# Transformer trunk on one core: VectorE work ordered behind the convolution, and a mixture gather with the one-hot matrix stationary

## The chip, the core and the metric

The kernel runs on one core of a Trainium2 chip. The metric is device time in microseconds of one execution. Engines are named as in the profile: PE (TensorE), PEld (its weight load), DVE (VectorE), ACT (ScalarE), POOL (GpSimd), SP (SyncE, whose queue issues nearly all transfers). Everything is float32; "fp32r" is the reduced form of it that TensorE takes in one pass, and the kernel writes an fp32 value as a sum of two such parts, hi and lo, where one is not enough.

## The reference

Two layers over x (512 positions, 1024 channels). The first layer mixes by a Fourier group and a convolution group, the second by windowed attention; after each comes an expert-choice mixture. Every sub-layer starts with RMSNorm and a shift, scale and gate made from the conditioning vector c ("adaLN").

```python
def adaln(cond, w, b):
    shift, scale, gate = jnp.split(cond @ w + b, 3, axis=-1)

def fourier_conv_mixer(h, ...):              # layer 0
    proj = h @ w_in                          # u_f, u_v, u_g: 512 channels each
    y_f = real(fft2(u_f in 4 groups of 128)) # positions x channels
    glu = u_v * sigmoid(u_g)
    conv = depthwise_conv(glu, width 31) + conv_b
    y_c = silu(layer_norm(conv))
    return concatenate([y_f, y_c]) @ w_out

def ec_moe(h, ...):                          # both layers, 16 experts, 64 rows each
    aff = softmax(h @ router_w + router_b)
    gate, idx = top_k(swapaxes(aff), 64)     # each expert picks its 64 positions
    xg = h[idx]
    hid = silu(xg @ w_gate) * (xg @ w_up)    # 1024 x 1024 per expert
    return zeros.at[idx].add((hid @ w_down) * gate)

x = x + gate * mixer(h); x = x + gate * ec_moe(h)    # per layer, h = norm, scale, shift
```

## The kernel before

The program is unrolled Python. A scheduler orders each engine's queue from program order and its own estimate of durations. Two things override it: `behind(i)`, which puts the instructions traced inside it behind instruction i on the engine of i, and a manual order for PE that follows program order from the second pair of experts on.

**Slots.** Most transfers go to eleven buffers of 1 MiB ("w") and, at times, four more (3a, 3b, 4a, 4b), taken and given back in turn (`Slot`). SP's queue is in order, so a transfer whose buffer is not free holds up the ones behind it. "0a", "0b", "1a", "1b", "2a", "2b" are larger areas that several stages use one after another.

**Layer 0's mixer** (`mixer0`, L409) is written as a list of tokens (L616). Of these, `g` makes a gated input of the convolution (`gated`, L539), `c` a convolution of one of four 128-channel tiles (`conv`, L500), `F` and `s` the Fourier group, `D` and `E` an adaLN block (`ada_block`, or `ada_steps` if the token ends in d or p), `O` a half of the output weights split in hi and lo, `y` the hi and lo of one Fourier tile, `L`, `M`, `N` the LayerNorm over channels and swish, `e` and `m` the first and the second half of an output tile's matmuls, `B` the gate row, `T` the router's preparation (`Router(0)`), `r` its logits. The letter behind the dot is the engine that makes the lo parts: v for DVE, g for POOL.

**The convolution.** Tile 1 is made on ACT and POOL. Tiles 0, 3 and 2, in this order, are made on DVE: 31 taps each (L519, L522), every one a multiply-add of 128x512 that reads the running sum from a PSUM bank and writes it back. L then needs all four tiles: a sum over channels on PE (L602), the mean (L673), the subtraction (L675), squares, a second sum, the inverse root, and swish; then the lo and hi parts of the result (L588, L589) and the second halves of the output matmuls (L150 to L152).

**An adaLN block** multiplies c with 1024x512 weights on PE (L236), turns the row to columns (L296), adds them up on DVE (L298) and adds the bias on DVE (L299). `ada_steps` does the multiply on DVE or ACT and POOL instead, in eight steps (L275, L277) that are dealt out between the tokens that follow.

**The mixture** (`moe`, L905) takes experts in eight pairs. For a pair: gather the 128 rows (two experts of 64) through a one-hot matrix; gate and up (`expert_mm`, L1011), each 2 MiB a step in four steps; hid = silu(gate) * up, turned (L1118); down; combine (L1060: the transposed one-hot matrix times hi and lo of the result, added into x by DVE at L1063). While a pair's up is done, the next pair is gathered: `onehot` (L943) builds the 0/1 matrix on DVE and multiplies it by the norm's factor r on POOL (L955); `gather` (L959) takes 128x128 pieces of the frozen x ("0a", "0b") as the stationary operand and the one-hot matrix as the moving one, 32 fp32 matmuls of 128 columns, and scales and shifts each result (L972 on ACT, L974 on DVE) into one of two buffers "1b", "2b". `weights` (L977) turns the one-hot matrix for the combine (L983) and picks the affinities (L988). The expert weights of a layer are 16 x 3 x 4 MiB, read once.

## Time and profile before

| | us |
|---|---|
| median of 3 runs | 1469.9 |
| lowest and highest | 1465.23, 1471.7 |
| profiled execution, its own time | 1466.26 |
| its span in the trace | 1464.6 |

The span is taken from the first to the last instruction in the trace, and 1.7 us lie around it. Slices 8 to 18 (257 to 690 us) are the first mixture, 27 to 39 (985 us to the end) the second; before each stands a mixer, with PE, DVE, ACT and POOL at work on one chain of steps. An engine's busy share is a mean over these stages. PE's clock is printed as a share of 2.4 GHz; 0.5 is the lower of its two levels, 1.2 GHz.

### The profile page before, as it was taken

What the parts mean: (1) busy time and instruction counts of PE and PEld (TensorE: products, weight loads), DVE (VectorE), ACT (ScalarE), POOL (GpSimd) and SP (SyncE); (2) the same over time, 40 slices, a digit from 0 to 9 for tenths busy, and PEclk for the clock granted to TensorE, in tenths of its full rate; (3) what the DMA queues carried; (4) which work ended last, traced back from release to release, by engine and by line L of the source; (5) the groups of instructions that cost most, each with busy time, mean ns of one, the idle gap of its engine ahead of it and who ended that gap; (6) DMA issues with size and microseconds to landing.
All of it is one profiled execution on the core that took longest, in us unless ns stands there. A gap on an engine that the chain in (4) does not pass through costs nothing.

```text
span 1464.6 us, 18139 instructions
## 1 busy us (share of the span) xinstructions
PE 1361.0 (93%) x7235; PEld 771.0 (53%) x7235; DVE 593.3 (41%) x1170; ACT 337.1 (23%) x686; POOL 285.4 (19%) x234
## 2 busy tenths in 40 slices
PE   5999698999999999999798989979999999999995
PEld 3785475545455355354476666655454554553543
DVE  5589547121222212211477988671122222222214
ACT  3365232110010010010356543421100010010002
POOL 2488131200000000000256654410000000000002
PEclk8999797999999999999999989989999999999998
DMA  9469469979999999999800375688799999999995
GB/s 337 130 218 350 139 232 412 396 315 397 423 421 422 421 423 422 422 422 410 271 29 30 113 232 165 238 330 336 321 396 424 421 422 422 422 421 422 421 410 172
DMA packets 112860, 480.69 MB, mean 328 GB/s; under 512 B 10416, under 2 KB 31176, under 8 KB 67208
## 3 DMA queue, kind: packets, MB, share of 16 engines
q1 hardware_dynamic: 112696, 479.27, 82.9%
q8 instruction: 57, 0.93, 0.3%
q0 software_dynamic: 80, 0.26, 0.0%
q14 instruction: 27, 0.22, 0.0%
HBM read 477.40 MB, written 2.10 MB: 327 GB/s over the span
## 4 chain that ended last, share of the span: by engine, by line
PE 63%; DMA 20%; DVE 11%; ACT 3%; issue 1%; SPq 1%; POOL 1%; DVEq 0%; ACTq 0%; POOLq 0%
PE bank L1022 31%; PE bank L966 7%; DMA w<-in_moe_w_up_dram 5%; DMA w<-in_moe_w_gate_dram 5%; DMA w<-in_moe_w_down_dram 4%; PE bank L150 4%; PE bank L151 4%; PE bank L152 4%; PE bank L1060 3%; PE bank L1043 3%; PE bank L1352 1%; DVE bank L522 1%; PE bank L236 1%; DMA 4b<-in_moe_w_gate_dram 1%; DMA 4a<-in_moe_w_up_dram 1%
## 5 line engine op out<-in xcount | busy, mean ns | idle before, releaser
L1022 PE MATMUL bank<-w,area2b 128*64 128x512 f32 x736 | 187.0, 594 | 3.4 <-DMA w<-in_moe_w_up_dram 2.1
L1022 PE MATMUL bank<-w,area1b 128*64 128x512 f32 x704 | 181.7, 594 | 3.4 <-DMA w<-in_moe_w_up_dram 2.1
L1022 PE MATMUL bank<-w,area1a 128*64 128x512 f32 x632 | 161.5, 594 | 2.6 <-ACT area1a L162 1.2
L1063 DVE TENSOR_TENSOR x<-x,bank 128x512 f32<-128x512 f32 (+1 forms) x136 | 78.8, 650 | 176.1 <-PE bank L1060 176.1
L955 POOL TENSOR_TENSOR tmp<-tmp,rr 128x512 f32<-128x512 f32 x14 | 17.4, 1244 | 580.5 <-DVE tmp L949 558.8
L1022 PEld LDWEIGHTS bank<-w,area2b 128*64 128x64 f32 x736 | 62.3, 137 | 99.0 <-issue 85.2
L1022 PEld LDWEIGHTS bank<-w,area1b 128*64 128x64 f32 x704 | 60.3, 137 | 99.0 <-issue 85.0
L1053 DVE SCALAR_TENSOR_TENSOR tmp<-bank,af,gbc 128x512 f32<-128x512 f32 (+1 forms) x34 | 24.4, 719 | 211.5 <-PE bank L1022 184.7
L1113 DVE TENSOR_TENSOR area1a<-bank,area1a 128x512 f32<-128x512 f32 x32 | 22.0, 691 | 209.7 <-PE bank L1022 209.7
L128 POOL TENSOR_TENSOR w<-w,w 128x1024 fp32r<-128x1024 f32 x30 | 72.8, 2444 | 145.9 <-DMA 3b<-in_ada_w_dram 120.2
L1022 PEld LDWEIGHTS bank<-w,area1a 128*64 128x64 f32 x632 | 54.3, 137 | 76.1 <-issue 69.6
L1060 PE MATMUL bank<-area2a 128*128 128x512 f32 (+1 forms) x272 | 64.6, 387 | 6.4 <-ACT area2a L1054 6.4
L1054 ACT ACTIVATE area2a<-tmp 128x512 fp32r<-128x512 f32 (+1 forms) x34 | 20.6, 607 | 213.0 <-DVE tmp L1053 212.9
L1060 PEld LDWEIGHTS bank<-area2a 128*128 128x128 f32 x272 | 47.9, 188 | 30.3 <-ACT area1a L1089 9.7
L966 PE MATMUL bank<-tmp,0a 128*128 128x128 f32 x384 | 62.2, 285 | 0.0
L1089 ACT ACTIVATE area1a<-bank 128x512 f32<-128x512 f32 x32 | 19.1, 598 | 186.1 <-PE bank L1022 186.1
L966 PE MATMUL bank<-tmp,0b 128*128 128x128 f32 x384 | 61.0, 282 | 0.0
L150 PE MATMUL bank<-area1a,w 128*128 128x512 f32 x132 | 52.7, 418 | 5.8 <-ACT area1a L386 3.7
L966 PEld LDWEIGHTS bank<-tmp,0a 128*128 128x128 f32 x384 | 52.7, 196 | 9.7 <-issue 9.7
L972 ACT ACTIVATE area1b<-bank,mod 128x128 f32<-128x128 f32 x32 | 14.6, 457 | 179.1 <-DVE area1b L974 179.1
L152 PE MATMUL bank<-area1a,w 128*128 128x512 f32 x132 | 53.1, 404 | 1.2 <-POOL w L128 1.2
L151 PE MATMUL bank<-area2a,w 128*128 128x512 f32 x132 | 53.1, 402 | 0.1
(478 smaller groups left out, 2610.3 us busy)
## 6 DMA issues: line engine op xcount, KB each, us to landing
w<-in_moe_w_gate_dram SPq DMA_DIRECT2D x95, 1024.0 KB, 16.8
w<-in_moe_w_up_dram SPq DMA_DIRECT2D x85, 1024.0 KB, 19.7
w<-in_moe_w_down_dram SPq DMA_DIRECT2D x84, 1024.0 KB, 18.4
w<-in_ada_w_dram SPq DMA_DIRECT2D x42, 1024.0 KB, 5.7
4a<-in_moe_w_up_dram SPq DMA_DIRECT2D x10, 1024.0 KB, 12.3
3b<-in_moe_w_up_dram SPq DMA_DIRECT2D x10, 1024.0 KB, 17.1
3a<-in_moe_w_up_dram SPq DMA_DIRECT2D x9, 1024.0 KB, 15.6
4b<-in_moe_w_down_dram SPq DMA_DIRECT2D x9, 1024.0 KB, 16.1
```

Of the source, the lines that this page charges most:

```text
L128: eng.tensor_sub(lo.ap[:, s], w.ap[:, s], hi.ap[:, s].bitcast(FT))
L150: nc.tensor.matmul(ps, l[0], r[0], start=start, stop=False)
L151: nc.tensor.matmul(ps, l[0], r[1], start=False, stop=False)
L152: nc.tensor.matmul(ps, l[1], r[0], start=False, stop=stop)
L966: nc.tensor.matmul(p[:, P * q:P * q + P], src_x(t, 4 * hf + q), oh[:, P * t:P * t + P], start=t == 0, stop=t == TT - 1)
L1022: nc.tensor.matmul(ps[h][CAP * i:CAP * i + CAP], lhs[:, k, CAP * i:CAP * i + CAP], w[i].row(kk)[:, 512 * h:512 * h + 512], start=k == 0, s ...
L1043: nc.tensor.matmul(ps[CAP * i:CAP * i + CAP, :n], lhs[:, k, CAP * i:CAP * i + CAP], w[i][:, kk], start=k == 0, stop=k == KT - 1)
L1053: nc.vector.scalar_tensor_tensor(f, ps[:, :n], af, gbc[:, s], op0=OP.mult, op1=OP.mult)
L1054: nc.scalar.activation(Y[0][:, s], f, AF.Copy)
L1060: nc.tensor.matmul(p[:, :n], ohT[:, P * t:P * t + P], Y[z][:, c0:c0 + n], start=z == 0, stop=z == 1)
L1063: nc.vector.tensor_add(xx, xx, p[:, :n])
L1113: nc.vector.tensor_mul(sg[:, s], ps, sg[:, s])
```

## The change

Around the convolution, the blocks D1, D0, D2, D4, D5 and D3 no longer add their bias (`bias=False`). Two additions do it for all of them (`ada_bias`), at B and at T. These, the whole of `Router(0)` and the eight DVE steps of block E3 are put behind the convolution's last tap on DVE (`behind(*ended)`). The lo parts of O1, y3 and y2 go from DVE to POOL. Tile 2 is convolved ahead of tile 3.

In both mixtures, from the third pair on, the gather is `Rows`. During the up of pair n (n = 1 to 6), behind each of its four steps, PE multiplies the one-hot matrix of pair n+1 (now fp32r, and the stationary operand) with hi and lo of two 128x512 pieces of the frozen x, which ACT (hi) and DVE (lo) have just split. That is 16 matmuls of 512 columns. A half's sum is copied out of PSUM by ACT, turned by four PE transposes, and scaled and shifted as before. The first half is turned behind up, the second behind hid's transposes. The frozen x carries the factor r already, so POOL's multiplication of the one-hot matrix falls away. There is one buffer for the gathered rows of all pairs from the second on, and one for hid; "1b" and "2b" hold hi and lo.

```diff
-    def ada_block(l, s, j, room=None, fast=False):
+    def ada_block(l, s, j, room=None, fast=False, bias=True):
...
+    def ada_bias(l, s, c0, n):
+        m, b0 = mod[l, s][:, c0:c0 + n], 8 + (2 * l + s) * 24 + c0
+        return nc.vector.tensor_add(m, m, colsA[:, b0:b0 + n])
...
-                nc.vector.tensor_add(cv, acc, cv)
+                tap = nc.vector.tensor_add(cv, acc, cv)
+            ended[:] = [tap]
...
-        toks = ("p3 p0 p2 p1 p5 p4 g0 F0 g1 w:21 g2 s0:1 g3 D1:3 F2 F3 n F1 c0.0 D0:04 c1.30 c3.0 s2 D2:1 c2.0 s1 D4 "
-                "L D5:12 D3:22 s3:2 H O2.g:004 y0.g O0.g:033 M O1.v:01 N0.v y1.g O3.g y3.v y2.v N1.v e4 N2.v e0 e1 e3 "
+        toks = ("p3 p0 p2 p1 p5 p4 g0 F0 g1 w:21 g2 s0:1 g3 D1:3 F2 F3 n F1 c0.0 D0:04 c1.30 c2.0 s2 D2:1 c3.0 s1 D4 "
+                "L D5:12 D3:22 s3:2 H O2.g:004 y0.g O0.g:033 M O1.g:01 N0.v y1.g O3.g y3.g y2.g N1.v e4 N2.v e0 e1 e3 "
...
+        def after_conv(f):
+            def step():
+                with behind(*ended):
+                    f()
+            return step
...
-                drip += ada_steps(*(todo if op == 'D' else more)[j], arg == "p")
+                steps = ada_steps(*(todo if op == 'D' else more)[j], arg == "p")
+                drip += steps if arg == "p" else [after_conv(f) for f in steps]
...
-                ada_block(*todo[j], "0a" if arg else None)
+                ada_block(*todo[j], "0a" if arg else None, bias=False)
...
             elif op == 'B':
+                with behind(*ended):
+                    ada_bias(0, 0, 16, 8)
                 row_bcast(gbc, mod[0, 0][:, 16:24])
...
             elif op == 'T':
-                rt = Router(0)
+                with behind(*ended):
+                    ada_bias(0, 1, 0, 16)
+                    rt = Router(0)
...
-        hids = [kview(A1[:, 1024 + 1024 * i:2048 + 1024 * i]) for i in range(2)]
-        xgs = [kview(area(m, 1024)) for m in ("1b", "2b")]
+        hid = kview(A1[:, 2048:3072])
+
+        xgs = [kview(area("1b", 1024)), kview(A1[:, 1024:2048])]
...
+        class Rows:
...
+            def __init__(self, pr):
+                onehot(pr)
+                self.xg, self.oh = xgs[1], ohs[pr % 2]
+                if not stage:
+                    stage.extend(area(m, 1024, FR) for m in ("1b", "2b"))
+                self.rows = []
+
+            def step(self, c):
+                hf = c // 2
+                if c % 2 == 0:
+                    self.bank = Bank()
+                    self.p = self.bank.__enter__()
+                for t in range(2 * (c % 2), 2 * (c % 2) + 2):
+                    hi, lo = (stage[t % 2][:, 512 * z:512 * z + 512] for z in range(2))
+                    x = frozen[2 * t + hf]
+                    nc.scalar.activation(hi, x, AF.Copy)
+                    nc.vector.tensor_sub(lo, x, hi.bitcast(FT))
+                    for z, m in enumerate((hi, lo)):
+                        nc.tensor.matmul(self.p, self.oh[:, P * t:P * t + P], m, start=t + z == 0,
+                                         stop=t + z == TT)
+                if c % 2:
+                    f = tmp()
+                    nc.scalar.activation(f, self.p, AF.Copy)
+                    self.bank.__exit__()
+                    self.rows.append(f)
+
+            def turn(self, hf):
+                with Bank() as p:
+                    for q in range(4):
+                        nc.tensor.transpose(p[:, P * q:P * q + P], paired(self.rows[hf], q), ident)
+                    modulate(self.xg, p, hf, range(4))
...
-                expert_mm([u0, u1], xg, wu_d, e, None, None if pr else "u")
+                rows = None
+                if 0 < pr < NP - 1:
+                    rows = Rows(pr + 1)
+                expert_mm([u0, u1], xg, wu_d, e, None, None if pr else "u", rows and rows.step)
...
-                elif pr + 1 < NP:
-                    onehot(pr + 1)
-                    nxt = ahead()
+                elif rows:
+                    rows.turn(0)
+                    nxt = weights(pr + 1)
...
+            if rows:
+                rows.turn(1)
...
-                            nc.gpsimd.tensor_copy(frozen[2 * t + h], xx)
+                            nc.gpsimd.tensor_scalar(frozen[2 * t + h], xx, r, None, op0=OP.mult)
                         else:
-                            nc.scalar.activation(frozen[2 * t + h], xx, AF.Copy)
+                            nc.scalar.activation(frozen[2 * t + h], xx, AF.Copy, scale=r)
```

## Rows read from the trace of the kernel before

**Rows 1.** The page: busy time of each engine, and GB/s in 40 equal slices

```profile
PE 1361.0 (93%) x7235; PEld 771.0 (53%) x7235; DVE 593.3 (41%) x1170; ACT 337.1 (23%) x686; POOL 285.4 (19%) x234
...
GB/s 337 130 218 350 139 232 412 396 315 397 423 421 422 421 423 422 422 422 410 271 29 30 113 232 165 238 330 336 321 396 424 421 422 422 422 421 422 421 410 172
```

**Rows 2.** Windows inside the first mixture; busy time (instructions) by engine, clock, DMA share, GB/s

```profile
400.00:545.00 145.00, 143.83 (x776) 73.61 (x777) 33.80 (x58) 14.11 (x27) 4.07 (x3) 1.00 1.01 422
545.00:685.00 140.00, 135.11 (x672) 66.40 (x668) 30.02 (x52) 11.23 (x21) 1.06 (x1) 1.00 1.01 421
```

**Rows 3.** Chain of work that ended last, 540 to 720: start, length, what

```profile
545.97 19.77 DMA w<-in_moe_w_up_dram
...
685.88 3.66 PE bank L1022 x14
```

**Rows 4.** The same chain through one pair of experts, 395 to 470

```profile
399.76 7.74 PE bank L966 x64
407.50 0.44 PE bank L983 x4
...
410.24 27.69 PE bank L1022 x128
437.93 3.89 PE bank L1060 x16
441.82 13.88 PE bank L1022 x64
```

**Rows 5.** Windows where the weight stream has gaps

```profile
355.00:360.00 5.00, 5.00 (x26) 1.61 (x24) 0.00 (x0) 0.00 (x0) 0.00 (x0) 1.00 0.70 241
1090.00:1095.00 5.00, 4.57 (x22) 1.96 (x24) 0.33 (x1) 0.71 (x2) 0.00 (x0) 1.00 0.68 285
```

**Rows 6.** Timeline of DVE, 60 to 250: start, length, what, [idle before, releaser]

```profile
96.38 0.69 DVE L537 TENSOR_TENSOR 3b<-bank,tmp 128x512 f32<-128x512 f32 x1 [2.85 <-PE bank L152]
...
97.95 11.05 DVE L522 SCALAR_TENSOR_TENSOR bank<-3b,cw,bank 128x512 f32<-128x512 f32 x14
...
123.01 0.69 DVE L589 TENSOR_TENSOR area2a<-0a,area1a 128x512 fp32r<-128x512 f32 x1 [2.13 <-ACT area1a L588]
...
137.18 1.91 DVE L331 SCALAR_TENSOR_TENSOR a<-mod,colsC 128x4 f32<-128x4 f32 x1
...
139.67 1.90 DVE L763 TENSOR_TENSOR aw<-rw,a 128x128 f32<-128x128 f32 x1
...
160.33 0.75 DVE L522 SCALAR_TENSOR_TENSOR 0b<-3b,cw,bank 128x512 f32<-128x512 f32 x1
166.35 2.48 DVE L675 TENSOR_TENSOR 0b<-0b,bank 128x512 f32<-128x512 f32 x4 [5.27 <-PE bank L673]
```

**Rows 7.** Groups by line, DVE, 122.5 to 161.2: busy, mean ns, idle before

```profile
L275 DVE SCALAR_TENSOR_TENSOR w<-w,sil 128x512 f32<-128x512 f32 x6 | 4.5, 750 | 0.0
L331 DVE SCALAR_TENSOR_TENSOR a<-mod,colsC 128x4 f32<-128x4 f32 x2 | 2.6, 1282 | 0.0
```

**Rows 8.** Who waited for whom, 130 to 165

```profile
PE bank L602 <- DVE 0b L522: 12.2, 1, 12.2
```

**Rows 9.** Windows before and after the convolution's last tap (161.1), and around it

```profile
135.00:161.10 26.10, 10.34 (x47) 6.63 (x39) 25.86 (x37) 6.95 (x9) 6.29 (x4) 0.74 0.63 206
161.10:190.20 29.10, 27.27 (x126) 18.78 (x126) 7.67 (x20) 13.82 (x21) 8.35 (x7) 0.94 0.56 203
190.20:220.00 29.80, 29.80 (x167) 24.01 (x167) 14.58 (x20) 7.46 (x17) 10.55 (x8) 1.00 0.52 192
160.00:165.00 5.00, 3.87 (x9) 1.85 (x10) 1.04 (x2) 0.60 (x1) 0.00 (x0) 0.51 0.00 0
```

**Rows 10.** Timeline of POOL, 130 to 180

```profile
136.71 4.71 POOL L128 TENSOR_TENSOR w<-w,w 128x1024 fp32r<-128x1024 f32 x2
```

**Rows 11.** Instructions on tile tmp, 320 to 680: ns minimum/median/maximum

```profile
L1054 ACT ACTIVATE area2a<-tmp x12: 630/632/634, 368.3 to 655.1; 128x512 fp32r<-128x512 f32 x12
L1055 DVE TENSOR_TENSOR area2a<-tmp,area2a x12: 681/690/1530, 369.6 to 655.8; 128x512 fp32r<-128x512 f32 x12
```

More of the change, by code (lines that the diff above doesn't have):

```diff
@@ L255, in ada_block @@
                 nc.scalar.activation(rows, ps, AF.Copy)
-        return ada_cols(l, s, j, rows)
+        return ada_cols(l, s, j, rows, bias)
     def ada_steps(l, s, j, pool_too=False):
@@ L291, in ada_steps, with ada_cols @@
                 [lambda k=k: add(k) for k in range(4, 8)] + [finish])
-    def ada_cols(l, s, j, rows):
+    def ada_bias(l, s, c0, n):
+        m, b0 = mod[l, s][:, c0:c0 + n], 8 + (2 * l + s) * 24 + c0
+        return nc.vector.tensor_add(m, m, colsA[:, b0:b0 + n])
+    def ada_cols(l, s, j, rows, bias=True):
         with Bank() as pc:
@@ L296, in ada_cols @@
                 nc.tensor.transpose(pc[:, P * q:P * q + P], rows[:, P * q:P * q + P], ident)
-            b0, m = 8 + (2 * l + s) * 24 + 4 * j, mod[l, s][:, 4 * j:4 * j + 4]
-            nc.vector.reduce_sum(m, pc.rearrange("p (q g i) -> p q g i", q=4, g=4)[:, :, :, 0], axis=AX.X)
-            return nc.vector.tensor_add(m, m, colsA[:, b0:b0 + 4])
+            nc.vector.reduce_sum(mod[l, s][:, 4 * j:4 * j + 4],
+                                 pc.rearrange("p (q g i) -> p q g i", q=4, g=4)[:, :, :, 0], axis=AX.X)
+            return ada_bias(l, s, 4 * j, 4) if bias else None
     def ada(l, s, blocks):
@@ L521, in conv @@
                 else:
-                    nc.vector.scalar_tensor_tensor(out, g[:, k:k + S], wt(k), acc, op0=OP.mult, op1=OP.add)
+                    tap = nc.vector.scalar_tensor_tensor(out, g[:, k:k + S], wt(k), acc, op0=OP.mult, op1=OP.add)
             if split:
-                nc.vector.tensor_add(cv, acc, cv)
+                tap = nc.vector.tensor_add(cv, acc, cv)
+            ended[:] = [tap]
         todo = [(0, 0, 4), (0, 0, 5)] + [(0, 1, j) for j in range(4)]
@@ L530, in mixer0 @@
         tiles = [(w, P * j) for j in range(2) for w in w0] + [(wf0, P * j) for j in range(2)]
-        sum_bank = []
+        sum_bank, ended = [], []
         def glu_of(ct, pg, pv):
@@ L920, in moe @@
         sg = A1[:, 0:1024]
-        hids = [kview(A1[:, 1024 + 1024 * i:2048 + 1024 * i]) for i in range(2)]
-        xgs = [kview(area(m, 1024)) for m in ("1b", "2b")]
+        hid = kview(A1[:, 2048:3072])
+        xgs = [kview(area("1b", 1024)), kview(A1[:, 1024:2048])]
+        A2b = area("2b", 1024)
+        stage = []
         Y, ohTs = [], []
@@ L945, in onehot @@
             e = 2 * pr
-            ohs[pr % 2] = oh = tmp()
+            ohs[pr % 2] = oh = tmp(FR if pr > 1 else FT)
             if pr == 0:
@@ L959, in gather @@
         def gather(pr, hf):
[L961 removed]
+            xg, oh = xgs[pr], ohr[0]
             for qs in ((0, 1), (2, 3)) if pr == 0 else (range(4),):
@@ L965, in gather @@
                         for t in range(TT):
-                            nc.tensor.matmul(p[:, P * q:P * q + P], src_x(t, 4 * hf + q),
+                            nc.tensor.matmul(p[:, P * q:P * q + P], paired(x_sb[:, t], 4 * hf + q),
                                              oh[:, P * t:P * t + P], start=t == 0, stop=t == TT - 1)
-                    for q in qs:
-                        k = 4 * hf + q
-                        pp = p[:, P * q:P * q + P]
-                        if q % 2:
-                            nc.scalar.activation(xg[:, k], pp, AF.Identity, bias=sh[:, k:k + 1], scale=a[:, k:k + 1])
-                        else:
-                            nc.vector.tensor_scalar(xg[:, k], pp, a[:, k:k + 1], sh[:, k:k + 1],
-                                                    op0=OP.mult, op1=OP.add)
+                    modulate(xg, p, hf, qs)
@@ new lines, in modulate @@
+        def modulate(xg, p, hf, qs):
+            for q in qs:
+                k = 4 * hf + q
+                pp = p[:, P * q:P * q + P]
+                if q % 2:
+                    nc.scalar.activation(xg[:, k], pp, AF.Identity, bias=sh[:, k:k + 1], scale=a[:, k:k + 1])
+                else:
+                    nc.vector.tensor_scalar(xg[:, k], pp, a[:, k:k + 1], sh[:, k:k + 1], op0=OP.mult, op1=OP.add)
+        class Rows:
[28 more added lines that the diff above has]
+                    modulate(self.xg, p, hf, range(4))
@@ L977, in weights @@
         def weights(pr):
             e, oh, ohT = 2 * pr, ohs[pr % 2], ohTs[pr % 2]
-            o = [oh[:, P * t:P * t + P] for t in range(TT)]
+            o = [(oh.bitcast(FT) if pr > 1 else oh)[:, P * t:P * t + P] for t in range(TT)]
             with Bank() as p:
@@ L1009, in back, with expert_mm @@
                 pass
-        def expert_mm(ps, lhs, wd, e, middle=None, first=None):
+        def expert_mm(ps, lhs, wd, e, middle=None, first=None, after=None):
             for c in range(4):
@@ L1025, in expert_mm @@
                 back(w)
+                if after:
+                    after(c)
         def down_piece(ps, lhs, e, c0, n):
@@ L1091, in moe @@
                 combine_all(pend)
-            def ahead():
-                gather(pr + 1, 0)
-                gather(pr + 1, 1)
-                return weights(pr + 1)
             if pr == 0:
@@ L1130, in moe @@
             if pr == 0:
-                nxt = ahead()
+                gather(1, 0)
+                gather(1, 1)
+                nxt = weights(1)
                 frozen.extend(fourths("0a", "0b"))
```

11 lines of the change are left out of this document (4 added, 7 removed).

## The prediction

> **What bounds the kernel now.** Read the page first, then each stage by itself. The page has PE busy for 93% of the span, so a change that takes matmul time away looks as if it paid everywhere [rows 1]. The GB/s line beside it speaks against that: in both mixtures the transfers run at 421 to 423 GB/s for most slices and hardly ever above [rows 1]. So the second view is windows inside the first mixture. From 400 to 685 us the DMA share is 1.01 throughout, and PE's busy time is misleading: it stands at 143.8 of 145 and then 135.1 of 140 us, but the instructions per microsecond fall from 776/145 = 5.35 to 672/140 = 4.80 [rows 2]. The third view, the chain of work that ended last, says when that begins: from 546 on it runs through weight transfers of 19.8 us each, and PE works off what has just landed [rows 3].
>
> One pair of experts shows why. On PE a period goes from one gather to the next: 399.76 to 441.82 + 13.88 = 455.70, that is 55.94 us [rows 4]. The stream has to bring 24 MiB (2 experts, 3 matrices, 4 MiB each), 25.17 MB, which at 422 GB/s [rows 2] is 59.6 us. So DMA is the slower of the two by 3.7 us a pair; PE leads the chain only while the buffers, filled earlier, last. What counts in a mixture is therefore (a) when the stream starts and (b) where it has gaps.
>
> The other stage is the first mixer. There the view is the waits: PE stands for 12.2 us at the channel sum (L602) for DVE's last tap [rows 8], and from 135 to 161.1 us PE is busy 10.3 of 26.1 us while DVE is busy 25.9 [rows 9]. The timeline of DVE shows that it isn't only convolving there: between its taps stand router preparation (L331, L763), lo parts (L589) and E3's steps (L275) [rows 6, 7]. Here VectorE is the bound, and all that follows starts later for it.
>
> **The change: the convolution.** Taps run at 11.05/14 = 0.789 us each [rows 6]. The last two tiles need 62 of them, 48.9 us. In the trace the first of these tiles starts at 96.38 + 0.69 = 97.07, after 2.85 us of idleness for its gated input, and the last tap ends at 161.08 [rows 6]: 64.0 us for 48.9 us of taps. The other 15.1 us are what the change takes out: E3's eight steps (six of them 4.5 us), L331 2.6 [rows 7], L763 1.9, the lo parts of O1 (L128), L589 with its wait 2.8 [rows 6], and the bias additions, of the same kind as these small ones. Tile 2 ahead of tile 3 starts at once, at 93.53, since its input was made earlier. There remain the gated product of tile 3 (0.69) and six small sums, for which I take 1 us. So the last tap ends at 93.5 + 48.9 + 0.7 + 1.0 = 144.1, 17.0 us earlier.
>
> PE must be there to use it. Its 10.3 us of work between 135 and 161.1 [rows 9] stand ahead of the channel sum in its queue; without waits they end at 145.7. That is later than 144.1, so the sum starts 15.4 us earlier, not 17.0. Behind it PE is busy 27.3 of 29.1 us up to 190.2 [rows 9]: no cover is left there, and the whole of it moves as a block. The clock adds something: from 160 to 165 us the granted clock is 0.51, the lower level, behind a window in which PE was busy for 10.3 of 26.1 us [rows 9]; without such a pause the 3.9 us of matmuls in that window run at the higher level, worth up to 2 us.
>
> What was taken out must still be done. About 9 us of it (E3, L331, L763, two bias additions) goes to DVE behind the last tap. DVE is busy only 7.7 of the 29.1 us that follow [rows 9], and its first step on the chain, L675, has 5.3 us of idleness ahead of it [rows 6]. DVE's queue is in order, so each step of the chain can stand behind one moved step, 0.75 us [rows 7]; three such places cost 2.2 us, which I set against the clock. POOL gets O1's two lo parts (4.7 us, as the pair at 136.71 [rows 10]) and two Fourier tiles; it ends its own part of this stage at 141.4 [rows 10] and would end near 149, while the first matmuls on these come behind the LayerNorm. E3's transfers and buffers come at about the absolute time at which they came before. Sum: -15 us, between -8 (moved steps and POOL late at every place) and -20 (all of PE's 15.8 idle us, the clock, the 1.8 us at 190).
>
> Does it reach the end? From 190.2 to 220 us PE is busy without a pause [rows 9], with the output matmuls that need this chain's result, and the router and the first gather need theirs. The weight stream is no obstacle: it moves 206, 203 and 192 GB/s in these three windows [rows 9], half its rate, and waits for buffers that this stage holds. So both mixtures start earlier by the full amount.
>
> One row speaks against giving POOL more. L331 on 128x4 took 1.91 us and L763 on 128x128 took 1.90 us; both ended within 0.2 us of one of POOL's two subtractions, which fill 136.71 to 141.42 [rows 6, 10]. The Trainium skill ("SBUF — State Buffer", section "SBUF: two separate sides") gives a rule for it: VectorE and GpSimd share one pair of ports as an exclusive lock, so an operation of VectorE with two SBUF inputs blocks for the whole of GpSimd's. The trace agrees. By that rule E3's steps, which read two SBUF operands, would be held by O1's lo parts, and the sum would be -10 instead of -15; I don't take it, since taps, with one operand in PSUM, ran at 0.75 beside POOL.
>
> **The change: the gather.** Before, 7.74 us of PE a pair [rows 4]. After: 16 matmuls of 512 columns with an fp32r operand, as the combine's 16, 3.89 us, and eight transposes at 0.44 for four, 0.88 [rows 4]. So PE gains 2.97 us a pair, 12 times: 35.6 us in all. Nearly all of it is free time already: the stream takes 59.6 us where PE now takes 53.0. It pays only in the gaps of the stream behind the first new gather. There is one in each mixture, behind the second pair's up, when no buffer comes free during the gather: 0.30 and 0.32 of 5 us [rows 5], 1.5 and 1.6 us. Down now starts up to 3 us earlier, but the buffers of up are given back up to 2.9 us later, since three of the four steps stand between its matmuls. I take -2 for both mixtures, between 0 and -3.
>
> ACT and DVE get eight splits a pair, 0.63 and 0.69 us [rows 11], against 13.9 us of up [rows 4]; they run ahead of PE, with two sets of buffers. The waits that this adds (the first step behind the combine's additions, hid behind fewer matmuls) I put at 0 to 3 us a pair, inside the margin below.
>
> **The rivals.** (1) *PE is the bound and all its savings arrive.* For: 93% busy. Against: the instruction rate and the 1.01. Time: 1466.3 - 15 - 35.6 = 1416. (2) *The moved work ends last instead:* E3 and the router's preparation stand ahead of the chain on DVE, and POOL's lo parts hold it. For: the two rows of 1.9 us. Price: 9 us of DVE's work and more waiting, so that -15 becomes -2 to -8: 1458 to 1466. (3) *Slower: the splits stop PE.* Each of the eight splits is a step ACT, DVE, PE; if none ran ahead, they would cost 8 x (0.63 + 0.69) = 10.6 us a pair [rows 11]. Where it decides: in the first mixture the last up would end, without waits for DMA, at 441.82 + 4 x 55.94 + 13.88 = 679.5 [rows 4] and ends at 689.5 [rows 3], so PE has 10 us of cover, and 6 x 2.97 more: 28 us, 4.6 us a pair. At 10.6 it costs 6 x 6.0 = 36 us in each mixture, and the time is 1466 - 15 + 72 = 1523; from 6 us a pair on the kernel is slower than before. Against: two buffers, and 3.5 us of up between steps.
>
> **How the numbers follow.** The profiled execution took 1466.3 us, the median of the runs is 1469.9, 3.6 above. 1466.3 - 15 - 2 = 1449.3, and 3.6 for the median: 1453. Chances: forecast (1445 to 1462) 0.75; rival 2 0.15; rival 3 0.06; rival 1 0.04. The range takes the forecast's bounds, -20 - 3 and the spread of runs below, and most of rival 2 above: 1445 to 1464. About 0.5%, 7.3 us, is what a measurement can tell from no change. Faster by more than that (under 1462.5): 0.75 + 0.04 + 0.06 of rival 2 = 0.85; within: 0.09; slower: 0.06.
>
> **What would show it.** Right: the last tap near 144 and the channel sum on PE near 146, no wait of some 12 us for L522; what stands at 190 us and behind it some 15 us earlier; in the mixtures 422 GB/s as before, chain through transfers earlier than 546 - 15, instructions on PE fewer and the period still 59.6. Wrong: a last tap past 150, L675 waiting for L275 or for POOL, a DMA share under 1.0 behind the third pair (PE waiting for splits), or mixtures shorter by more than 3 us each.

## The result, and the profile after

The changed kernel takes 1451.35 us (median of four runs, 1450.2 to 1453.43) where the kernel before takes 1469.51: a ratio of 0.9885, 95% interval 0.9869 to 0.9902, 18 us less. The profiled execution took 1450.2 us, with a span of 1448.5, against 1466.3 and 1464.6. Forecast were 1453, faster, by 15 us in the convolution and 2 in the gather.

The page of the changed kernel, busy time of the engines and GB/s in 40 slices, against [rows 1]:

```profile
PE 1339.6 (92%) x6755; PEld 717.8 (50%) x6755; DVE 639.7 (44%) x1258; ACT 404.5 (28%) x806; POOL 286.4 (20%) x226
...
GB/s 329 136 207 333 269 246 403 336 405 417 422 421 423 422 422 421 422 421 396 211 30 29 115 235 195 212 375 337 315 419 423 421 422 422 422 421 422 422 409 167
```

PE is busy 21 us less, and the two plateaus of 421 to 423 GB/s are as before. Windows inside the first mixture (columns as in [rows 2]):

```profile
400.00:545.00 145.00, 139.64 (x642) 59.42 (x640) 43.52 (x75) 24.81 (x45) 0.00 (x0) 1.00 1.01 422
545.00:672.00 127.00, 116.95 (x536) 48.67 (x534) 32.65 (x58) 19.04 (x36) 0.00 (x0) 1.00 1.01 421
```

DMA stays at 1.01 and PE has fewer instructions and more idleness: what the gather gave back is waiting time. The chain of work that ended last, changed kernel, from the first gather on (start, length, what):

```profile
239.03 6.83 PE bank L983 x58
...
317.58 3.58 PE bank L1076 x16
...
371.19 3.58 PE bank L1076 x16
374.78 1.11 PE bank L1017 x4
...
397.25 14.74 DMA w<-in_moe_w_gate_dram
412.06 19.77 DMA 4a<-in_moe_w_up_dram
...
671.60 3.66 PE bank L1076 x14
...
973.23 6.83 PE bank L983 x58
```

The chain meets the transfers at 397, where it met them at 546 [rows 3]; a quarter of up (3.58) and a gather step (1.11) take turns. A pair takes 371.19 - 317.58 = 53.6 us of this chain, where it took 55.94 before [rows 4]. The timeline of DVE in the stretch that the convolution fills, changed kernel, against [rows 6] (lines are each kernel's own):

```profile
94.18 0.81 DVE L523 TENSOR_SCALAR bank<-3b,cw,colsC 128x512 f32<-128x512 f32 x1
...
97.00 0.69 DVE L542 TENSOR_TENSOR 3b<-bank,tmp 128x512 f32<-128x512 f32 x1 [1.21 <-PE bank L152]
...
110.36 0.17 DVE L301 TENSOR_REDUCE mod<-bank 128x4 f32<-128x16 f32 x1 [0.93 <-PE bank L300]
...
126.17 0.17 DVE L301 TENSOR_REDUCE mod<-bank 128x4 f32<-128x16 f32 x1 [3.83 <-PE bank L300]
...
141.47 0.18 DVE L301 TENSOR_REDUCE mod<-bank 128x4 f32<-128x16 f32 x1 [1.09 <-PE bank L300]
...
151.06 0.75 DVE L526 SCALAR_TENSOR_TENSOR 0b<-3b,cw,bank 128x512 f32<-128x512 f32 x1
...
152.28 0.23 DVE L335 SCALAR_TENSOR_TENSOR a<-mod,colsC 128x4 f32<-128x4 f32 x2
...
156.94 2.48 DVE L688 TENSOR_TENSOR 0b<-0b,bank 128x512 f32<-128x512 f32 x4 [0.48 <-PE bank L686]
```

The last tap ends at 151.06 + 0.75 = 151.8, 9.3 us earlier, not 17. The idle times in brackets say why: VectorE now stands for the adaLN sums. Who waited for whom, the same line of both kernels, DVE from 60 to 165 us, before and then after:

```profile
DVE mod L298 <- PE bank L296: 0.7, 1, 0.7
```

```profile
DVE mod L301 <- PE bank L300: 6.3, 4, 3.8
```

and PE's wait at the channel sum, after, in place of the 12.2 us of [rows 8]:

```profile
PE bank L607 <- DVE 0b L526: 4.5, 1, 4.5
```

Five events cut every trace into stages: the end of VectorE's last tap of tile 0 (its first of three), the end of its last tap of all, the start of the first gather, the last 14 matmuls of up in the first mixture (671.60 in the chain above), and the second mixture's first gather. All runs of the study stand here together: the length of each stage in the profiled execution in us, the span, and the median of the runs.

| kernel | up to these tiles | last two tiles | to first gather | first mixture | second mixer | from second gather | span | median |
|---|---|---|---|---|---|---|---|---|
| before | 93.5 | 67.6 | 89.7 | 435.1 | 301.6 | 477.1 | 1464.6 | 1469.5 |
| after | 94.2 | 57.7 | 87.2 | 432.6 | 301.6 | 475.3 | 1448.5 | 1451.4 |
| e1_conv_only | 94.2 | 57.7 | 87.2 | 434.1 | 300.2 | 477.0 | 1450.3 | 1452.6 |
| e2_gather_only | 93.5 | 67.6 | 89.1 | 433.1 | 303.4 | 474.7 | 1461.4 | 1467.1 |
| e4_extra1 | 93.3 | 57.7 | 86.4 | 437.1 | 304.2 | 479.8 | 1458.5 | 1460.1 |
| e4_extra2 | 93.0 | 57.7 | 88.8 | 455.5 | 301.2 | 502.2 | 1498.5 | 1502.4 |
| e3_act_evicts | 93.1 | 51.0 | 98.2 | 433.7 | 305.0 | 472.4 | 1453.4 | 1457.6 |
| e8_act_order | 93.2 | 50.9 | 89.5 | 432.4 | 307.6 | 475.4 | 1449.1 | 1451.4 |
| e9_order_alone | 92.8 | 57.6 | 90.3 | 432.4 | 302.6 | 474.5 | 1450.2 | 1453.7 |
| e10_rpart_pool | 94.2 | 50.9 | 89.7 | 432.7 | 304.3 | 475.9 | 1447.7 | 1449.2 |
| e5_e3_unordered | 94.6 | 64.9 | 86.9 | 432.1 | 304.0 | 474.6 | 1457.1 | 1459.6 |
| e7_lo_on_dve | 94.2 | 61.7 | 88.6 | 433.0 | 302.6 | 474.5 | 1454.6 | 1455.4 |
| e6_old_tile_order | 93.4 | 57.2 | 89.0 | 432.3 | 306.1 | 472.5 | 1450.5 | 1450.3 |

The first column is nearly the same code in all of them and runs from 92.8 to 94.6: so much do single executions differ ahead of the change. The stages behind don't contain that shift, but have a spread of their own. With the same code there, the last tap to the first gather takes 86.4 to 88.8 us (after, e1, both e4) and 89.1 to 89.7 (before, e2). A mixture with the new gather takes 432.1 to 433.7 us as the first and 472.4 to 475.9 as the second. The change's 16.1 us of span are 9.9 in the last two tiles, 2.5 from there to the first gather, 2.6 in the first mixture, 1.8 behind the second mixer, less 0.6 of the first column. The second mixer is edited by none of them but e10, and yet its length runs from 300.2 to 307.6.

### The profile page after: what moved, and what is told of

Same layout as the page of the kernel before. It is cut to its first block, busy times and chain, and to the rows that moved or that the text cites. A ratio compares the mean times of both kernels' runs of the same rounds, so it can differ in the third digit from the quotient of the medians.

```text
span 1448.5 us, 17484 instructions
## 1 busy us (share of the span) xinstructions
PE 1339.6 (92%) x6755; PEld 717.8 (50%) x6755; DVE 639.7 (44%) x1258; ACT 404.5 (28%) x806; POOL 286.4 (20%) x226
## 4 chain that ended last, share of the span: by engine, by line
PE 56%; DMA 31%; DVE 8%; ACT 2%; issue 1%; SPq 1%; POOL 0%; ACTq 0%; DVEq 0%; POOLq 0%
PE bank L1076 22%; DMA w<-in_moe_w_gate_dram 9%; DMA w<-in_moe_w_up_dram 7%; DMA w<-in_moe_w_down_dram 6%; PE bank L150 4%; PE bank L151 4%; PE bank L152 4%; DMA 4a<-in_moe_w_up_dram 3%; PE bank L1099 3%; PE bank L236 2%; PE bank L1116 2%; PE bank L983 2%; PE bank L1017 2%; DMA 3b<-in_moe_w_down_dram 1%; DMA 4a<-in_moe_w_down_dram 1%; DMA 4b<-in_moe_w_gate_dram 1%
## 5 line engine op out<-in xcount | busy, mean ns | idle before, releaser
L1076 PE MATMUL bank<-w,area1a 128*64 128x512 f32 x1936 | 496.6, 596 | 24.8 <-DMA w<-in_moe_w_gate_dram 23.3
L1076 PEld LDWEIGHTS bank<-w,area1a 128*64 128x64 f32 x1936 | 158.3, 137 | 277.7 <-issue 221.8
L128 POOL TENSOR_TENSOR w<-w,w 128x1024 fp32r<-128x1024 f32 x32 | 76.8, 2425 | 432.4 <-ACT w L127 429.2
L1076 PE MATMUL bank<-4b,area1a 128*64 128x512 f32 x184 | 83.7, 595 | 1.3 <-DMA 4b<-in_moe_w_gate_dram 1.3
L1076 PE MATMUL bank<-3a,area1a 128*64 128x512 f32 x184 | 84.1, 596 | 0.0
L1076 PE MATMUL bank<-3b,area1a 128*64 128x512 f32 x176 | 79.8, 595 | 1.3 <-DMA 3b<-in_moe_w_gate_dram 1.3
L1076 PE MATMUL bank<-4a,area1a 128*64 128x512 f32 x176 | 79.7, 595 | 1.3 <-DMA 4a<-in_moe_w_gate_dram 1.3
L1015 DVE TENSOR_TENSOR area1b<-0b,area1b 128x512 fp32r<-128x512 f32 x24 | 16.6, 693 | 77.4 <-ACT area1b L1014 43.5
L1014 ACT ACTIVATE area1b<-0b 128x512 fp32r<-128x512 f32 x24 | 15.1, 631 | 124.5 <-PE bank L1017 124.5
L526 DVE SCALAR_TENSOR_TENSOR bank<-3b,cw,bank 128x512 f32<-128x512 f32 x58 | 43.8, 755 | 1.8
L1015 DVE TENSOR_TENSOR area1b<-0a,area1b 128x512 fp32r<-128x512 f32 x24 | 16.6, 693 | 60.0 <-PE bank L1017 36.8
```

Of the source, the lines that this page charges most:

```text
L128: eng.tensor_sub(lo.ap[:, s], w.ap[:, s], hi.ap[:, s].bitcast(FT))
L526: tap = nc.vector.scalar_tensor_tensor(out, g[:, k:k + S], wt(k), acc, op0=OP.mult, op1=OP.add)
L1015: nc.vector.tensor_sub(lo, x, hi.bitcast(FT))
L1076: nc.tensor.matmul(ps[h][CAP * i:CAP * i + CAP], lhs[:, k, CAP * i:CAP * i + CAP], w[i].row(kk)[:, 512 * h:512 * h + 512], start=k == 0, s ...
```

## The experiments

**The two parts by themselves.** The convolution's part, with the gather as before:

```diff
-        xgs = [kview(area("1b", 1024)), kview(A1[:, 1024:2048])]
+        xgs = [kview(area(m, 1024)) for m in ("1b", "2b")]
...
+            def ahead():
+                gather(pr + 1, 0)
+                gather(pr + 1, 1)
...
-                    rows = Rows(pr + 1)
```

> Only the part around the convolution; both mixtures as in the kernel before. Theory (the mixtures are set by the weight stream; the convolution's part is worth what stands at the first gather, 11.7 us in the trace): 1469.5 - 11.7 = 1458, first gather near 239, and the gap of 1.5 us in the stream behind the third pair's gather back in both mixtures. Rival (PE is the bound, and the gather's 35.6 us of PE time count): the convolution's part alone would then be the whole gain less what the gather gives; with 18 us in all it could give nothing, or the kernel would be near 1469.

Measured: 1452.58 us, ratio to before 0.9882, interval 0.9857 to 0.9908. That is some 5 us below what I expected. Of the 14.3 us of span, 11.8 come up to the first gather, 1.0 in the first mixture and 1.4 in the second mixer.

And the gather's part alone, everything of the convolution as before:

```diff
-            xg, oh = xgs[pr % 2], ohr[0]
+            xg, oh = xgs[pr], ohr[0]
...
+        class Rows:
...
+                for t in range(2 * (c % 2), 2 * (c % 2) + 2):
...
+                    nc.scalar.activation(hi, x, AF.Copy)
+                    nc.vector.tensor_sub(lo, x, hi.bitcast(FT))
```

> Only the gather with the one-hot matrix stationary; the first mixer as in the kernel before. Theory: the gather's 2.97 us a pair show in PE's busy time (some 21 us less on the page) and only 3 to 4 us in the end: 1466. The shares show at the third pair's down, 1.5 to 2 us in each mixture. Rival (PE is the bound): 1469.5 - 35.6 = 1434.

Measured: 1467.12, ratio 0.9981, interval 0.9965 to 0.9997. The 35.6 us of PE don't arrive: the rival that PE is the bound falls. What does arrive can be seen in place. The window of 5 us in which e1's stream has its gap behind the third pair's gather, e1 first, the changed kernel second:

```profile
345.00:350.00 5.00, 5.00 (x26) 1.68 (x24) 0.00 (x0) 0.00 (x0) 0.00 (x0) 1.00 0.74 262
```

```profile
345.00:350.00 5.00, 5.00 (x26) 1.58 (x23) 0.00 (x0) 0.00 (x0) 0.00 (x0) 1.00 0.95 390
```

From 340 to 350 e1's stream (0.96 in the first 5 us, 0.74 in the second) lacks (1.01 - 0.96) x 5 + (1.01 - 0.74) x 5 = 1.6 us, and its first mixture is 1.5 us longer than the changed kernel's. In the second mixture, from 1075 to 1085, e1's shares are 0.85 and 0.83, 1.7 us lost, and the changed kernel's 0.99 and 1.01; there e1 is 1.7 us longer. So the gather is worth the gap that it closes, once in each mixture.

**What PE's time costs in the mixture.** The changed kernel, with the new gather's hi and lo matmuls done again into a bank that nothing reads, once (+3.9 us of PE a pair, six pairs a mixture) or twice (+7.8):

```diff
+                    with Bank() as d:
+                        for _ in range(1):        # 2 in e4_extra2
+                            for m in (hi, lo):
+                                nc.tensor.matmul(d, self.oh[:, P * t:P * t + P], m, start=True, stop=True)
```

> The changed kernel with every gather matmul from the third pair on done three times instead of once, the two additional ones into a bank that nobody reads: 32 more matmuls a pair, 7.8 us of PE. In the first mixture the last up ends at 675.3 and would end, without waits for the stream, at 371.2 + 5 x 53.6 + 14.3 = 653.5, so PE has 21.8 us of cover over six pairs, 3.6 us a pair. Theory: 6 x 7.8 - 21.8 = 25 us in each mixture, 1501. Rival (PE is the bound already): 2 x 6 x 7.8 = 93 us, 1545. Rival (the cover is larger, since PE's waits of each step hide the additional ones too): under 1475.

> The changed kernel with the hi and lo gather matmuls from the third pair on done twice (the second set into a spare bank that nothing reads): +3.9 us of TensorE per pair, 12 pairs. Theory (each pair has some 3.6 us of cover under the weight stream, as e4_extra2 showed with +7.8 us a pair): 1 to 4 us slower, 1452 to 1456 us. Rival (TensorE bounds the mixtures and every added microsecond pays): +47 us, 1498 us.

Measured: 1502.44 for +7.8 (ratio to before 1.0224, 1.0193 to 1.0255), as expected; 1460.06 for +3.9, 8.7 us above the changed kernel and outside what I expected of it. If PE were the bound these were +93 and +47. If each pair had cover of its own, +3.9 had cost next to nothing. It cost 4.5 us of 23.4 in each mixture (437.1 and 479.8 against 432.6 and 475.3); +7.8 cost 23.0 and 26.9 of 46.7. Windows of e4_extra1 say where:

```profile
340.00:345.00 5.00, 4.92 (x30) 2.73 (x32) 2.58 (x8) 1.86 (x4) 0.00 (x0) 1.00 0.81 331
345.00:350.00 5.00, 5.00 (x26) 1.59 (x23) 0.00 (x0) 0.00 (x0) 0.00 (x0) 1.00 0.72 241
```

Behind the third pair's gather, where PE still leads the chain, the stream stands again: from 330 to 355 its share is 0.89, 3.0 us lost; from 355 to 674 it is 1.01. In the second mixture it is 0.92 and 0.48 from 1080 to 1090, 3.1 us lost. The rest of the 4.5 us was not located. Cover is not so much a pair. At the third pair there is nearly none, later it is enough for 3.9 us and not for 7.8.

**Why the last tap came at 151.8.** If the waits for the adaLN sums are the cause, VectorE must not do these sums. In e3 TensorE itself takes one row of each group with a column of ones and zeros (`ind`), and ScalarE copies the 128x4 result:

```diff
+            if not bias:
+                for q in range(4):
+                    nc.tensor.matmul(pc[:, q:q + 1], rows[:, P * q:P * q + P], ind, start=True, stop=True)
+                return nc.scalar.activation(mod[l, s][:, 4 * j:4 * j + 4], pc[:, 0:4], AF.Copy)
```

> The changed kernel, with the six adaLN blocks beside the convolution summed on PE (four matmuls of the row with a column of ones at the four row groups, one column each, in place of the transposes) and copied out of PSUM by ACT, so that no step of DVE stands between the taps. Theory: DVE's waits of 6.3 us for the transposes go, and the last tap ends near 145 instead of 151.8; PE waits 4.5 us for that tap now, so 4 to 5 us of it arrive: 1447. Rival (something else is just as late: PE's own work, the tile on ACT and POOL, or ACT, which now waits for these sums): last tap earlier, but the time within 1.5 us of 1451.

Measured: 1457.6, ratio 0.9911, 0.9885 to 0.9937: slower than the changed kernel, a miss of 10 us, and outside the rival's range too. The first half of the theory holds. DVE has no wait for a sum left, the last two tiles take 51.0 us, not 57.7, and the last tap ends at 144.0. The gain is gone when the first gather starts: from the last tap to it are 98.2 us, 11.0 more than in the changed kernel. Timelines of e3, PE, DVE, POOL and ACT:

```profile
146.97 1.04 PE L611 MATMUL bank<-0b,one 128*32 128x512 f32 x2
```

```profile
143.29 0.75 DVE L530 SCALAR_TENSOR_TENSOR 0b<-3b,cw,bank 128x512 f32<-128x512 f32 x1
143.95 4.04 DVE L295 TENSOR_TENSOR mod<-mod,colsA 128x8 f32<-128x8 f32 x2
```

```profile
138.55 9.41 POOL L128 TENSOR_TENSOR w<-w,w 128x1024 fp32r<-128x1024 f32 x4 [0.49 <-ACT w L127]
```

```profile
153.22 2.57 ACT L271 ACTIVATE w<-w,sil 128x512 f32<-128x512 f32 x4 [3.08 <-DMA w<-in_ada_w_dram]
155.69 0.61 ACT L697 ACTIVATE 3a<-0b 128x512 f32<-128x512 f32 x1
...
172.84 2.57 ACT L271 ACTIVATE w<-w,sil 128x512 f32<-128x512 f32 x4 [1.80 <-DMA w<-in_ada_w_dram]
175.43 1.28 ACT L712 ACT_TABLE_LOAD   x1
```

Three things meet the earlier block. PE, at work without a pause, comes to the channel sum at 146.97, 2.9 us behind the tap. The bias additions of 128x8 take 4.04 us and end at 147.99, with POOL's four lo parts at 147.96; in the changed kernel, behind POOL's end, they take 0.25. And on ScalarE the scalings of a streamed adaLN block (L271) stand in the queue ahead of the squares (L697) and of the swish (L712), each time waiting for a transfer that doesn't come earlier because the taps do.

To settle the last, e8 is e3 with these scalings behind the squares and behind the last swish, and e9 has this order alone:

```diff
+        def after_act(f, k):
+            def step():
+                with behind(*(squares if k < 6 else swishes)):
+                    f()
+            return step
...
-                drip += steps if arg == "p" else [after_conv(f) for f in steps]
+                drip += [after_act(f, k) if k in (1, 2, 3, 4, 6, 7, 8, 9) else f for k, f in enumerate(steps)] if arg == "p" else [after_conv(f) for f in steps]
```

> This is the kernel of e3_act_evicts (TensorE itself sums each adaLN block's rows, ScalarE copies the 128x4 result, VectorE has no adaLN sum to wait for) with one more edit: on ScalarE the scalings of the streamed adaLN blocks (L271 of the changed kernel) stand behind the squares (first half of a block) and behind the last swish (second half), where in e3 they stood ahead of them and waited for their transfer. Theory (ScalarE's in-order queue ate e3's gain): the squares start where the mean's subtraction ends its first tile, 2.5 us or more earlier than in e3, the table load of the swish follows the normalising products directly (in e3 it came 4.0 us after their first one), the first gather's operands are 5 to 7 us earlier than in e3 and 2 to 4 us earlier than in the changed kernel: 1445 to 1450 us. Rival (the transfers bound the stretch, whichever engine waits for them): the scalings only wait elsewhere and the first gather stays within 1 us of e3's 242.2; 1456 to 1458 us.

> The changed kernel with the order of ScalarE's scalings (L271) alone, behind the squares and behind the last swish; the adaLN sums stay on VectorE as in the changed kernel. Theory (the last tap at 151.8 sets the block in the changed kernel, and ScalarE's queue only becomes late once the tap is earlier): there the scalings cost at most the 1.5 us between the first normalising product's end and the first swish's start, so 1450 to 1452 us. Rival (ScalarE's queue already costs several us in the changed kernel): 1445 to 1448 us.

Measured: e8 1451.41 (ratio 0.9877, 0.9853 to 0.9901), e9 1453.68 (0.9895, 0.987 to 0.9919). ScalarE in e8:

```profile
151.63 0.63 ACT L703 ACTIVATE 3a<-0b 128x512 f32<-128x512 f32 x1 [1.34 <-DVE 0b L698]
...
168.47 1.28 ACT L718 ACT_TABLE_LOAD   x1
```

Squares 4.1 and table load 7.0 us earlier than in e3, and the first gather at 233.7, 8.5 us ahead of e3 and 5.3 ahead of the changed kernel (0.9 of it already ahead of the last two tiles), at least what the queue theory asks. The rival, that the transfers bind whoever waits, falls. In e9, with the tap where it was, the order gains nothing, and the time is outside both ranges; behind the tap stand 90.3 us, 1.5 more than the longest of the four traces with the changed kernel's code (88.8). So ScalarE's queue became the next bound only when the tap moved.

But e8's time is the changed kernel's. The 5.3 us are still there at the first mixture's end (666.1 against 671.6) and gone at the second mixture's first gather (973.7 against 973.2). So the second mixer was compared between e8 and e9, in whose traces its instructions stand in nearly the same order. Up to 863 us e8 keeps its lead of 6.3 us; then these rows differ, DVE and POOL of e8, and DVE of e9:

```profile
885.69 2.38 DVE L792 TENSOR_TENSOR tmp<-rw,mod 128x128 f32<-128x128 f32 x1
```

```profile
885.55 2.38 POOL L128 TENSOR_TENSOR w<-w,w 128x1024 fp32r<-128x1024 f32 x1 [1.57 <-ACT w L127]
```

```profile
891.97 0.28 DVE L788 TENSOR_TENSOR tmp<-rw,mod 128x128 f32<-128x128 f32 x1
```

In e8 the product began 0.14 us behind POOL's subtraction and took 2.38 us, in e9 0.23 us ahead of it and took 0.28. PE, which needs the product's sum, stood 4.78 us in e8 and 2.80 in e9. Behind the pause it ran at the lower clock in both, in e8 from 893.1 to about 904.7, 11.6 us, in e9 from 897.4 to about 903.8, 6.4 us. Windows of e8 and then of e9, in the columns of [rows 9]:

```profile
890.00:895.00 5.00, 1.94 (x9) 1.85 (x9) 4.82 (x11) 0.16 (x1) 2.92 (x2) 0.60 0.86 197
895.00:900.00 5.00, 5.00 (x23) 2.56 (x23) 1.95 (x9) 2.29 (x9) 0.33 (x1) 0.50 0.63 199
900.00:905.00 5.00, 5.00 (x22) 4.07 (x22) 1.79 (x4) 1.99 (x2) 1.04 (x1) 0.53 0.70 229
```

```profile
895.00:900.00 5.00, 2.64 (x11) 2.52 (x12) 4.76 (x14) 0.36 (x1) 4.53 (x3) 0.70 0.83 164
900.00:905.00 5.00, 5.00 (x29) 2.47 (x29) 2.18 (x10) 2.09 (x9) 0.23 (x1) 0.62 0.99 301
```

The lead is 6.3 us before the meeting, 4.3 behind the pause (893.67 against 897.97 at L285) and 2.0 when the clock is back in both. So in e10 GpSimd does this one product:

```diff
-            nc.vector.tensor_mul(f, rw[:, l], self.sh[:, :, None].to_broadcast([P, KT, NE]))
+            (nc.gpsimd if l else nc.vector).tensor_mul(f, rw[:, l], self.sh[:, :, None].to_broadcast([P, KT, NE]))
```

> The kernel of e8_act_order with one product of the second router (L792 of e8, a 128x128 product on VectorE) issued on GpSimd. Theory (in e8 VectorE's L792 took 2.38 us where e9's took 0.28, because it ran beside GpSimd's L128 at 885.55 to 887.93; TensorE then stood 4.8 us at L795 and ran at half clock until 904.5; together this cost e8 4.3 us of the 6.3 us it had in hand over e9): without that meeting the second mixture's first gather comes 2 to 5 us earlier than e8's 973.7, the end with it: 1446 to 1449 us, below the changed kernel's 1451.4. Rival (the gain is lost in the weight stream of the second mixture, whatever attention does): the time stays at e8's 1451 within 1 us though the first gather is earlier.

Measured: 1449.24 (1449.07 to 1451.41), ratio 0.9871, 0.9853 to 0.9889, 0.2 us above the theory's range. The second mixer is 3.3 us shorter than e8's, and the second mixture's first gather 1.9 us earlier, since this execution was 1.0 us later already ahead of the last two tiles. At the end e10 is 2.2 us below e8 and 2.1 below the changed kernel. The intervals overlap, so it isn't shown to be faster than either. Even here only 1.4 of the 4.2 us that the first gather is ahead of the changed kernel are left at the second one. PE's pause is now 2.16 us, but the lower level stands behind it for about as long as in e8, from 892.5 to about 902.7:

```profile
895.00:900.00 5.00, 5.00 (x29) 3.94 (x29) 3.46 (x11) 1.65 (x7) 1.67 (x2) 0.50 1.02 298
```

So e10 gave back the pause, 2.6 us of it; that a shorter pause gives back the clock as well is not shown by it.

The same meeting stands in two more traces, e4_extra1 (POOL's subtraction from 895.54) and e6 (from 889.63), and in no other:

```profile
895.62 2.41 DVE L782 TENSOR_TENSOR tmp<-rw,mod 128x128 f32<-128x128 f32 x1
```

```profile
889.96 2.20 DVE L782 TENSOR_TENSOR tmp<-rw,mod 128x128 f32<-128x128 f32 x1
```

**The other edits of the convolution's part**, each undone by itself in the changed kernel: the order that keeps E3's steps behind the last tap (e5), the lo parts of O1, y3 and y2 back on VectorE (e7), tile 3 ahead of tile 2 (e6).

```diff
-                drip += steps if arg == "p" else [after_conv(f) for f in steps]
+                drip += steps                                    # e5
...
-        ... O1.g:01 N0.v y1.g O3.g y3.g y2.g N1.v
+        ... O1.v:01 N0.v y1.g O3.g y3.v y2.v N1.v                # e7
...
-        ... c1.30 c2.0 s2 D2:1 c3.0 s1
+        ... c1.30 c3.0 s2 D2:1 c2.0 s1                           # e6
```

> The changed kernel without the order that puts the weighted products of the other streamed adaLN block (L275, L277) behind the conv's last tap; all else as changed. Theory (each of the 8 products that slips in among the taps moves the last tap by its 0.75 us, and the block with it): last tap up to 5 us later than 151.8, time 1452 to 1456 us. Rival (VectorE's waits for the adaLN sums, 6.3 us in four places, take the products in for nothing): last tap within 1 us, 1450 to 1452 us.

> The changed kernel with the low parts of one output weight and of y3 and y2 (L128, L594) back on VectorE, where they were before; all else as changed. Theory (work in VectorE's queue ahead of the last tap moves the tap by its own length): 2 low parts of 128x1024 and up to 2 of 128x512, which cost some 2 us and 0.7 us each on VectorE, move the last tap by 3 to 5 us and the end with it: 1454 to 1457 us. Rival (they fit into the waits for the adaLN sums): 1450 to 1452 us.

> The changed kernel with the conv's third and fourth channel tile back in the old order (tile 3 ahead of tile 2). Theory (VectorE stands for its gate's input where that tile is gated late, 2.85 us in the kernel before): last tap 1.6 to 2.9 us later than 151.8 and the time up by as much, 1452.5 to 1454.5 us. Rival (the wait for the gate is absorbed by the waits for the adaLN sums that follow): last tap within 0.5 us, 1451 us.

Measured: e5 1459.64, 8.3 us above the changed kernel, its last two tiles 7.2 us longer; e7 1455.40, 4.0 us above, tiles 4.0 us longer; e6 1450.32, tiles 0.5 us shorter and not longer, as its rival says. In e5 the direction is right and the size too small. DVE and POOL of e5:

```profile
145.69 2.22 DVE L275 SCALAR_TENSOR_TENSOR w<-w,sil 128x512 f32<-128x512 f32 x1
...
148.49 2.17 DVE L275 SCALAR_TENSOR_TENSOR w<-w,sil 128x512 f32<-128x512 f32 x1
```

```profile
140.09 10.02 POOL L128 TENSOR_TENSOR w<-w,w 128x1024 fp32r<-128x1024 f32 x4
```

Two of the eight products, those beside POOL's lo parts, took 2.2 us where the others took 0.73 to 0.75. In e7 the first of O1's lo parts, beside POOL's, took 2.18 us on VectorE and the second 1.21, and VectorE's waits for the sums are less than half:

```profile
DVE mod L301 <- PE bank L300: 2.7, 3, 1.5
```

In place of the longest of them a lo part (L594) waits 3.6 us for ScalarE. In e6 tile 3's gate does wait its 2.85 us again, and the waits for the sums shrink to 0.74 + 1.55 + 1.60 + 0.26 = 4.15 us: one wait takes the other's place.

## Point by point

**The bounds: right.** The stream binds both mixtures and VectorE the first mixer. The chain met the transfers earlier than asked for, and e2 and e4 exclude a PE bound.

**The last tap: wrong by 7.7 us**, 151.8 where the sum gave 144.1; 0.6 of it lies ahead of tile 2, and the last two tiles took 57.7 us for 50.6. The step that failed is "six small sums, for which I take 1 us". The gated product still waited, 1.2 us; the sums waited 6.3, and their own work is about half the 1 us. I priced them by their length, from a trace in which they waited 0.7 us. Much of what the change takes out stood in VectorE's queue ahead of the sums and gave PE time for its transposes: with the lo parts back there, in e7, the sums wait 2.7 us. The moved work was cover, and it went: of the 15.1 us taken out (2.1 of them L589's own wait for ScalarE [rows 6]), 6.3 came back as waits in the same queue. The lost cover is not all of it, for PE's own order changed too. The transposes of the second and longest wait (3.83), before and then after:

```profile
122.52 0.66 PE L296 MATMUL bank<-ident,w 128*128 128x128 f32 x4
```

```profile
125.47 0.66 PE L300 MATMUL bank<-ident,w 128*128 128x128 f32 x4
```

They come 2.95 us later, where this execution is 0.6 us later at 94: some 2.3 us of that wait are PE's. That these waits make the difference is shown by e3, e8 and e10, where the two tiles take 51 us, as in the sum. The 6.7 us between 57.7 and 51.0 are the 6.3 of waits and the sums' own work. The sign of error that I gave, a last tap past 150, came true.

**The block moves with the tap: right.** From the last tap to the first gather are 89.7 us before and 87.2 after, and in e5 and e7 tiles and time moved by like amounts. It holds only as long as the next bound is far. With the tap at 144.0 the first is PE, which comes to the channel sum at 146.97 in e3, where I had put 145.7; the second is ScalarE's queue, a step that the prediction didn't look at (e3, e8).

**The clock's 2 us: wrong here. The 2.2 us of moved steps: not paid at the mean.** The two stood against each other in the sum. The first 5 us behind the last tap, before and then after, in the columns of [rows 9], and PE's channel sum after:

```profile
161.10:166.10 5.00, 4.97 (x12) 2.47 (x13) 0.00 (x0) 1.19 (x2) 0.00 (x0) 0.62 0.00 0
```

```profile
151.80:156.80 5.00, 4.94 (x11) 2.46 (x12) 4.49 (x12) 3.04 (x6) 0.00 (x0) 0.66 0.39 144
```

```profile
151.86 1.87 PE L607 MATMUL bank<-0b,one 128*32 128x512 f32 x2 [4.48 <-DVE 0b L526]
```

PE still stands for the tap, 4.5 us, and the granted clock is still 0.50 behind it, until about 155.4. The term holds under its condition, "without such a pause": in e3 the clock at the sum is 1.00, the sum takes 1.04 us for 1.87, and from its start to the mean's subtraction are 3.8 us for 5.1. As for the moved steps, the mean's subtraction waits for PE (0.48), not for one of them. They became cheap besides: the router's two scalings take 0.23 us for 2.6 [rows 7] and its weights 0.29 for 1.90 [rows 6], since at 152 POOL has ended. From the last tap to the mean's subtraction are 5.1 us, before 5.3: of the 2.5 us gained between tap and gather 0.1 lies there. Where the rest lies wasn't followed, and 2.5 is hardly more than the 2.4 by which this stage differs with the same code.

**The rule that I weighed and didn't take.** Rows 1.91 and 1.90 [rows 6, 10], 4.04 in e3, 2.2 in e5, 2.18 in e7, 2.41 in e4_extra1, 2.20 in e6 and 2.38 in e8 show one thing: while POOL subtracts 128x1024, a VectorE operation that reads two SBUF operands stands until that subtraction ends, however small it is; the taps, which accumulate in PSUM, run at 0.75 beside it. That is the Trainium skill's rule ("SBUF — State Buffer", section "SBUF: two separate sides"), and the runs agree with it. A column scaling with one SBUF tensor is held too: the three of 128x384 behind the product (L1403 in e8, L1399 in e9) took 3.81 and 3.94 us, for 1.07 at 880.38 in e9. Around the changed kernel's last tap this costs nothing, because E3's steps and the bias additions begin at 151.7 and POOL ended at 149.0; my reason for leaving it out, that taps aren't held, was beside the point. It decides as soon as the block is earlier.

**Does it reach the end: right for this change.** 11.7 us at the first gather and 16.1 at the end. Not right in general: e8's lead was lost in the second mixer, 2.0 us by the held product and 2.3 while the lower clock behind it lasted longer, 11.6 us for 6.4, as compared with e9.

**The gather: right**, -1.5 and -1.7 us in the two mixtures between e1 and the changed kernel, for the gaps of 1.5 and 1.6 that I read [rows 5], in sum a little past the 0 to -3 that I gave. All runs with the new gather and no added matmuls lie below both with the old one (434.1 and 435.1, 477.0 and 477.1). PE itself gains 2.3 us a pair (55.94 to 53.6) and not 2.97: a gather step takes 1.11 us, four of them 4.4 for the 3.89 that I put. That term wasn't the one that pays. **The cover of 4.6 us a pair in rival 3 was mis-sized:** +3.9 us a pair already costs 4.5 us a mixture, because the third pair has nearly none.

**The sum.** -16.1 in the profiled execution for -17. It came near by luck in part: the front gave 11.7 and not 15, the gather 3.3 and not 2. Besides, the first mixture is 1.0 us shorter in e1 as well, with the old gather (its stream lacks 1.0 us less of transfers from 230 to 680 than before), which I hadn't put down and which is within the spread of that stage, 1.6 us. The clock and the moved steps, set against each other at 2 us, cancelled because neither came.

**What stays open.** The second mixer is 300.2 to 307.6 us long. Before, e2, e3, e5, e6, e8, e9 and e10 order its instructions in one way, after, e1, e4 and e7 in another, and 301.6 us stands in both groups. The traces with the held product have the longest second mixers of their order: e8 and e6 307.6 and 306.1, the others 301.6 to 305.0; e4_extra1 304.2, the others 300.2 to 302.6. Only the loss of e8 against e9 was followed to its rows; e3's 305.0, without such a meeting, stays open.

## What to carry to other kernels

Before work is taken out of an in-order queue, list the waits that it hides there, and price what then stands first by its producer's time, not by its own length. Follow a gain in a stage to the stage's end and through the next ones: here one of 7 us ended in another engine's queue, and one of 4 us in a meeting of two instructions 650 us later. Where a stream of weights binds, PE's time is worth the gaps it makes or closes, and these lie at the first pairs, where the buffers have no lead yet.

## What the runs showed that was not expected

- A VectorE product of 0.28 us (128x128, both operands in SBUF) took 2.38 us when it began 0.14 us behind a GpSimd subtraction of 128x1024, and 0.28 when it began 0.23 us ahead of one.
- Behind the 2.0 us that it lost another 2.3 went: PE, idle for 4.8 us, came back at a granted clock of 0.50 (1.2 GHz) and stayed there for 11.6 us; in e9, idle for 2.8 us, for 6.4. That the longer pause made the stretch longer is not shown: in e10, idle for 2.2 us, it is 10.2.
- 3.9 us of extra matmuls a pair, in a stage where the stream takes 59.6 us a pair and PE, from 317.58 to 371.19 in the chain, 53.6, cost 4.5 us of 23.4 a mixture; 3.0 us of gaps stand behind the first pair so changed.
